# A hybrid SSD / RWKV-7 / PEER decoder step on one Trainium2 core: GpSimd's products go to VectorE

## The chip, the core and the metric

The kernel runs on one core of one Trainium2 chip. A core has TensorE (PE: matrix products into PSUM), VectorE (DVE), ScalarE (ACT), GpSimd (POOL) and SyncE (SP), which issues most transfers. The engines have queues of their own and wait for each other by semaphores. The metric is the device time of one execution in microseconds, lower is better: 3061.49 us is the median of three runs before the change (3054.85 to 3067.48).

## The reference

One layer is computed for a prompt of 512 tokens and for 8 samples of one token each, D_MODEL 1024, all in float32:

```python
h = rmsnorm(x, norm_mix)
z, xbc_raw, dt_raw, rw_proj, gate_m, gate_r = split_proj(h @ w_in)
y_m = mamba_branch(...)   # causal conv, SSD scan in chunks of 128, 32 heads, gated group norm
y_r = rwkv_branch(...)    # token shift, RWKV-7 recurrence, 16 heads of 64, group norm, bonus, gate
x = x + (sigmoid(gate_m) * y_m + sigmoid(gate_r) * y_r) @ w_out
x = x + peer(rmsnorm(x, norm_ffn))   # 8 heads, top 16 of 128 x 128 experts each, gelu
x = x + sigmoid(rmsnorm(x, norm_ple) @ w_ple_gate) * (p @ w_ple_proj)
y = rmsnorm(x, norm_final)
```

The samples start from given states (SSD, convolution, RWKV, shift); all new states are outputs too. In `peer` the top 16 of each half's scores are combined to candidates, the top 16 of those give a pair of indices (i, j) and a softmax gate, and the expert's row in `peer_u` and `peer_v` is i * 128 + j.

## The kernel before

Float32 products are made from pairs: a value is split into a part rounded for TensorE (`hi`, a copy on ACT) and the rest (`lo`, a subtraction on DVE, line 79), and `mm3` (lines 95 to 97) multiplies hi by hi, lo by hi and hi by lo. Weights arrive in tiles of 128 columns through SP's queue, are split, and meet 2 x 260 columns of tokens (512 of the prompt, 8 of the samples).

**The mixer.** A loop over eight groups g. A group is 128 RWKV channels (two of the sixteen heads) and one of the eight SSD groups (four heads, 256 channels). For each group the code projects r, k and v (`rw_tile`: raw copy on ACT, then the difference to the token before, line 418, on POOL, then the mix, line 420, on DVE); `rwkv_in` makes the decays `dr`, `di`, `dp`, `de` on ACT, normalises k to `kk` (line 545), makes `bb = kk * a` on POOL (line 547), changes `a` in place on DVE (line 548), and makes `ar`, `bk` (DVE, lines 553 to 560) and `ck` (POOL, lines 561 and 562). `rwkv_inv` multiplies `ar` by `bk` on TensorE, sends 16x16 blocks through DRAM, inverts them row by row on DVE, and reads them back into `tc16`; from it come `T16` (the buffer `di`, DVE) and `TT16` (the buffer `dp`, POOL), both on line 610. `rwkv_pre` forms the inverses of 64x64 blocks from them (its first product, line 513, reads `dp`) and the masked products `AM`; a part of `AM` is then overwritten with `ar` by copies on POOL (line 671). `rwkv_chain` is the recurrence over eight chunks of 64: each passes TensorE, DVE, TensorE, ACT, TensorE, DVE. Between these steps stand the convolution and z projections and the SSD chunks (`ssd`): its state decay (line 994) and the gating by z (line 1008) are on POOL.

**The samples** of a group are generators (`rwkv_s`, `ssd_s`) that `step()` moves on by one piece after each projection of the next group; the first group has none beside it. They load states into `sB` and `sH` and update them with products over 128x512 (lines 834 to 843) and 128x1024 (lines 916 to 921), shared between DVE and POOL. For group 7 their transfers are issued from POOL's queue (`Qu`), otherwise from SP's.

**The look-up.** `pairs` finds the pair of each of 16 candidates per head: a comparison of 128x2048 on DVE (line 1362), a product with the index table on POOL (line 1364), a sum on DVE (line 1365); twice for each of five token blocks, ten in all. The block 3 is done first; the others run as generators beside the products of the expert table `peer_u` (`u_in`, `u_out`), and `scatter` places the gates with one-hot tiles (lines 1412 and 1416, DVE). Token block 3 gathers its experts' rows by indirect transfers from POOL's queue (line 1453, five buffers), used by DVE on lines 1462 and 1468.

**Order.** A planner puts each engine's instructions in order by priorities and its own estimates. `pin` (`keep_in_program_order`) holds an instruction behind the one that was written before it for the same engine; both halves of line 610, and lines 834, 836, 916 and 917, are pinned. Each engine's queue is then fixed and runs in order.

Of the kernel before, what the change touches and what calls it, by code (L numbers as in the profile page):

```python
# [30 lines left out]
def tile_hybrid(ctx: ExitStack, tc, x_prompt, x_sample, p_prompt, p_sample, state_ssm, state_conv,  # L31
# [381 lines left out]
    def rw_tile(j):  # L413

        ps = proj(W_RW + j * P, P, hT)
        raw = raw_of(ps, rwS[:, j], rtail[:, j:j + 1], 1)
        d = l2.tile([P, 2, NH], F32, name="dtmp").rearrange("p i t -> p (i t)")[:, :512]
        G.tensor_tensor(d, raw[:, 2:514], raw[:, 3:515], op=OP.subtract)
        xs = lp.tile([P, 512], F32, name=f"xs{min(j // 8, 2)}")
        V.scalar_tensor_tensor(xs, d, rows["shift_mu"][:, j:j + 1], raw[:, 3:515], op0=OP.mult, op1=OP.add)  # L420
        return xs
# [96 lines left out]
    def rwkv_in(g, r, k, v, lw_):  # L518

        ps = pb()  # L520
        T.matmul(ps, lhsT=lw_[64:128, 1], rhs=xa[64:128], start=True, stop=True)
        a = full("a")
        S.activation(a, ps, AF.Tanh, scale=0.5, bias=rows["aaa_a0"][:, g:g + 1])
        S.activation(a, a, AF.Copy, scale=0.5, bias=0.5)
        ps = pb()
        for b in range(4):
            T.matmul(ps[:, b * P:(b + 1) * P], lhsT=xwaug[:, b * P:(b + 1) * P], rhs=lw_[0:65, 0], start=True, stop=True)
        lw = full("lw")
        S.activation(lw, ps, AF.Tanh, scale=0.5)
        S.activation(lw, lw, AF.Copy, scale=-0.5 * CDEC, bias=-0.5 * CDEC)  # L530
        dr, di, dp_, de = full("dr"), full("di"), full("dp"), full("de")
        for m, outs in ((cumI, ((dr, 1.0), (di, -1.0))), (cumS, ((dp_, 1.0),)), (cumC, ((de, 1.0),))):
            ps = pb()
            for b in range(4):
                T.matmul(ps[:, b * P:(b + 1) * P], lhsT=lw[:, b * P:(b + 1) * P], rhs=m, start=True, stop=True)
            for o, sg in outs:
                S.activation(o, ps, AF.Exp, scale=sg)
        drc = l2.tile([P, 8], F32, name="drc")
        V.tensor_copy(drc, dr[:, 63:512:64])

        sq = full("sq")
        S.activation(sq, k, AF.Square, scale=rows["k_k"][:, g:g + 1])
        ps = head_rs(sq, 1e-12, bd64, pb)
        kk = full("kk")
        V.scalar_tensor_tensor(kk, k, rows["k_k"][:, g:g + 1], ps, op0=OP.mult, op1=OP.mult)
        bb = full("bb")
        G.tensor_tensor(bb, kk, a, op=OP.mult)
        V.tensor_scalar(a, a, rows["k_a"][:, g:g + 1], omka[:, g:g + 1], op0=OP.mult, op1=OP.add)
        k2 = full("k2")
        V.tensor_tensor(k2, k, a, op=OP.mult)  # L550
        V.scalar_tensor_tensor(sq, r, rows["r_k"][:, g:g + 1], k2, op0=OP.mult, op1=OP.mult)
        ar = lp.tile([P, 8, 2, 64], F32, name="ar", bufs=2)
        V.scalar_tensor_tensor(ar[:, :, 0, :], c8(kk), -1.0, c8(dp_), op0=OP.mult, op1=OP.mult)
        V.tensor_tensor(ar[:, :, 1, :], c8(r), c8(dr), op=OP.mult)
        bk = lp.tile([P, 8, 2, 64], F32, name="bk")
        ck = lp.tile([P, 8, 2, 64], F32, name="ck")
        for e in range(2):
            sl = slice(64 * e, 64 * e + 64)
            V.tensor_tensor(bk[sl, :, e, :], c8(bb)[sl], c8(di)[sl], op=OP.mult)
            V.tensor_tensor(bk[sl, :, 1 - e, :], c8(k2)[sl], c8(di)[sl], op=OP.mult)  # L560
            G.tensor_tensor(ck[sl, :, e, :], c8(bb)[sl], c8(de)[sl], op=OP.mult)
            G.tensor_tensor(ck[sl, :, 1 - e, :], c8(k2)[sl], c8(de)[sl], op=OP.mult)
        return drc, sq, ar, bk, ck

    def bonus(sq, v):
# [8 lines left out]
    def rwkv_inv(g, ar, bk):  # L574

        L64 = c8(full("de"))
        lc16 = lp.tile([P, 8, 16], F32, name="lw")
        for hf in range(2):
            hs = slice(4 * hf, 4 * hf + 4)
            L = mm4(lambda ro, i: ar[ro, 4 * hf + i, 0, :], lambda ro, i: bk[ro, 4 * hf + i, ro.start // 64, :])  # L580
            V.tensor_tensor(L64[:, hs], L, b64(m64, 4), op=OP.mult)
            lm = c8(full("kk"))[:, 0:4]
            V.tensor_tensor(lm, L, b64(m16, 4), op=OP.mult)
            V.tensor_reduce(lc16[:, hs], lm.rearrange("p c (b k) -> p c k b", k=16), axis=AX.X, op=OP.add)
        ld, td = ld_d[g % 2], td_d[g % 2]
        nc.scalar.dma_start(ld.rearrange("c p k -> p c k"), lc16)
        yield
        lb = lp.tile([64, 16, 16], F32, name="a")
        pin(nc.sync.dma_start(lb.rearrange("q r k -> q (r k)"), ld.rearrange("c (z r) k -> (c z) (r k)", r=16)))
        yield  # L590
        tb = lp.tile([64, 16, 32], F32, name="sq")
        pin(V.memset(tb, 0.0))
        V.memset(tb.rearrange("p r k -> p (r k)")[:, 0:512:33], 1.0)
        tf = lp.tile([64, 16, 16], F32, name="k2")
        for j in range(15):
            tt = tf[:, j + 1:, 0:j + 1]
            sh = [64, 15 - j, j + 1]
            i = V.tensor_tensor(tt, lb[:, j + 1:, j:j + 1].to_broadcast(sh), tb[:, j:j + 1, 0:j + 1].to_broadcast(sh), op=OP.mult)
            if j == 0:
                pin(i)  # L600
            V.tensor_tensor(tb[:, j + 1:, 0:j + 1], tb[:, j + 1:, 0:j + 1], tt, op=OP.add)
        S.copy(tb[:, :, 16:32], tb[:, :, 0:16].rearrange("p r k -> p k r"))
        nc.scalar.dma_start(td.rearrange("c (z r) k -> (c z) (r k)", r=16), tb.rearrange("q r k -> q (r k)"))
        yield
        tc16 = lp.tile([P, 8, 32], F32, name="lw")
        pin(nc.scalar.dma_start(tc16, td.rearrange("c p k -> p c k")))
        yield
        T16, TT16 = c8(full("di")), c8(full("dp"))
        for q, (E_, t) in enumerate(((V, T16), (G, TT16))):
            pin(E_.tensor_tensor(t.rearrange("p c (b k) -> p c b k", k=16),  # L610
                                 tc16[:, :, None, 16 * q:16 * q + 16].to_broadcast([P, 8, 4, 16]),
                                 mb16[:, None].to_broadcast([P, 8, 4, 16]), op=OP.mult))
        yield L64, T16, TT16

    def rwkv_pre(g, v, ar, bk, ck, L64, T16, TT16):
# [21 lines left out]
        for hf in range(2):  # L637
# [30 lines left out]
                S.copy(uv[rv, e], pv[rv])  # L668
            for e in range(2):
                ro = slice(64 * e, 64 * e + 64)  # L670
                G.tensor_copy(AM[ro, e, :, 0:64], ar[ro, 4 * hf:4 * hf + 4, 0, :])
            out.append((AM, TT64, ctok, uv))
        return out

# [94 lines left out]
    def rwkv_s(g, lw_):  # L769
# [63 lines left out]
        yield  # L833
        pin(V.tensor_tensor(t1, sw, nkk, op=OP.mult))
        V.tensor_reduce(sa, t1, axis=AX.X, op=OP.add)
        pin(G.tensor_tensor(sw, sw, dec, op=OP.mult))
        G.tensor_tensor(t2, kS, bl(v8, 64), op=OP.mult)
        V.tensor_tensor(t1, bS, bl(sa, 64), op=OP.mult)
        V.tensor_tensor(sw, sw, t1, op=OP.add)
        V.tensor_tensor(sw, sw, t2, op=OP.add)  # L840
        Qu(g).dma_start(wkv_sample[0].rearrange("b h v k -> b (h v) k")[:, gs].rearrange("b p k -> p b k"), sw)
        G.tensor_tensor(t2, sw, rS, op=OP.mult)
        V.tensor_reduce(yrS[:, g], t2, axis=AX.X, op=OP.add)

    def samples_out(l2):
# [31 lines left out]
    def ssd_s(g):  # L877
# [33 lines left out]
        for i in range(2):  # L911
# [1 line left out]
            hs_, t1 = (lp.tile([P, 8, P], F32, name="sH", bufs=2) for _ in range(2))  # L913
            pin(Qu(g).dma_start(hs_, sst[:, rs_].rearrange("b p n -> p b n")))
            yield
            pin(G.tensor_tensor(t1, Bb, bl(dx[:, i, 0:8], P), op=OP.mult))
            pin(V.tensor_tensor(hs_, hs_, bl(dx[:, i, 8:16], P), op=OP.mult))
            V.tensor_tensor(hs_, hs_, t1, op=OP.add)
            Qu(g).dma_start(sso[:, rs_].rearrange("b p n -> p b n"), hs_)
            G.tensor_tensor(t1, hs_, Cb, op=OP.mult)  # L920
            V.tensor_reduce(y2[:, i], t1, axis=AX.X, op=OP.add)
            if i == 0:
                yield
# [18 lines left out]
    def ssd(g, xt, bm, cm, sz):  # L942
# [9 lines left out]
        for c in range(4):  # L952
# [38 lines left out]
            T.matmul(ps[:, 0:256], lhsT=bt, rhs=xde, start=True, stop=True)  # L991
            st2 = l2.tile([P, 256], F32, name="sst")
            if c:
                G.tensor_tensor(v4(st2), v4(st), hb(elast, c), op=OP.mult)
                V.tensor_tensor(st2, st2, ps[:, 0:256], op=OP.add)
            else:
                S.copy(st2, ps[:, 0:256])
# [7 lines left out]
        nc.scalar.dma_start(ssm_prompt[0, 0].rearrange("h q n -> (h q) n")[g * 256:(g + 1) * 256].rearrange("(j p) n -> p j n", p=P), so)  # L1005

        for j in range(2):
            G.tensor_tensor(yf[j], yf[j], sz[j], op=OP.mult)
            S.activation(sz[j], yf[j], AF.Square)
        V.tensor_tensor(sz[0], sz[0], sz[1], op=OP.add)  # L1010
        yield
# [309 lines left out]
    def pairs(pool, c, gate):  # L1321
# [38 lines left out]
        for s_ in range(2):  # L1360
            eq = pool.tile([P, 8, 16, 16], F32, name="eq")[:n]
            V.tensor_tensor(eq, iota[:n, None, None, 0:16].to_broadcast([n, 8, 16, 16]),
                            ab[:, s_].unsqueeze(3).to_broadcast([n, 8, 16, 16]), op=OP.is_equal)
            G.tensor_tensor(eq, eq, fi[:, :, s_].unsqueeze(2).to_broadcast([n, 8, 16, 16]), op=OP.mult)
            V.tensor_reduce(ij[:, s_].rearrange("p (h k) -> p h k", h=8), eq, axis=AX.X, op=OP.add)
            yield
        V.tensor_tensor(gate, top, top[:, :, 0:1].to_broadcast([n, 8, 16]), op=OP.subtract)
# [349 lines left out]
```

## Time and profile before

| what | value |
|---|---|
| median of three runs | 3061.49 us |
| the profiled execution | 3051.57 us |
| its span, first to last instruction | 3049.9 us |
| TensorE busy, mean granted clock | 2821.5 us (93%), 0.954 |
| DVE busy | 2249.9 us (74%) |
| ACT busy | 988.6 us (32%) |
| POOL busy | 685.8 us (22%), 309.6 of it indirect transfers |

The granted clock is the share of TensorE's full clock that the chip allowed in a stretch. The mixer runs from the start to about 1200 us, the branch and output projections to about 1430, scores and look-up keys to 1560, the products with `peer_u` to about 2400, those with `peer_v` to 2954, and the last block to the end. Busy shares are means over stages with different limits.

### The profile page before, as it was taken

The page shows a single profiled execution, that of the slowest core. Times are in us where ns is not written, and L with a number is a line of the kernel's source. Part 1 is how long each engine was busy: PE and PEld are TensorE (multiplying, and loading weights), DVE is VectorE, ACT ScalarE, POOL GpSimd, SP SyncE. Part 2 cuts the span into 40 slices and gives each one's busy share as a digit, 9 for nine tenths or more (in the row PEclk, how much of TensorE's full clock was granted, in tenths as well). Part 3 has the DMA queues.
Part 4 walks back from the last instruction along what each step waited for, and adds up shares of the span by engine and source line. Part 5 has one row for each costly group of instructions (what it writes and reads, how often), then busy time and mean ns, then how long its engine had stood idle before and what let it go on. Part 6 is the DMA issues. An engine that isn't in the chain of part 4 may idle for free. (4 is left out here: it accounts for less than half of the span.)

```text
span 3049.9 us, 52517 instructions
## 1 busy us (share of the span) xinstructions
PE 2821.5 (93%) x20188; PEld 2617.4 (86%) x20192; DVE 2249.9 (74%) x5375; ACT 988.6 (32%) x1995; POOL 685.8 (22%) x522
## 2 busy tenths in 40 slices
PE   5999999898897999998968989899999999999998
PEld 4878888777777888987968989898999999999986
DVE  5867767787777775334999999695677778878846
ACT  2333323333242322332223333232323343333332
POOL 0222231322314132210013121121222333432100
PEclk9999979998988999999989999999999999999999
DMA  3314242424334265632326768677998989988830
GB/s 87 78 41 105 76 103 60 113 60 104 73 87 113 68 153 158 198 112 93 90 61 198 245 203 245 211 241 230 315 334 303 328 302 327 337 326 313 287 119 29
DMA packets 446995, 528.15 MB, mean 173 GB/s; under 512 B 95464, under 2 KB 357243, under 8 KB 446705
## 3 DMA queue, kind: packets, MB, share of 16 engines
q1 hardware_dynamic: 386153, 377.42, 40.1%
q0 software_dynamic: 38304, 139.22, 13.5%
q10 hardware_dynamic: 22288, 8.16, 1.1%
q8 instruction: 159, 2.61, 0.4%
q14 instruction: 91, 0.75, 0.1%
HBM read 447.83 MB, written 77.14 MB: 172 GB/s over the span
## 5 line engine op out<-in xcount | busy, mean ns | idle before, releaser
L97 PE MATMUL ps<-hhi,wlo 128*128 128x260 f32 (+1 forms) x1456 | 444.6, 305 | 1.7 <-DVE wlo L79 1.7
L96 PE MATMUL ps<-hlo,whi 128*128 128x260 f32 (+1 forms) x1456 | 444.4, 305 | 0.0
L95 PE MATMUL ps<-hhi,whi 128*128 128x260 f32 (+1 forms) x1456 | 443.8, 305 | 0.6 <-DVE rsa L122 0.3
L97 PE MATMUL psA<-h2h,ul 128*128 128x392 f32 x1024 | 354.1, 346 | 24.8 <-DVE ul L1500 24.4
L95 PE MATMUL psA<-h2h,uh 128*128 128x392 f32 x1024 | 365.7, 357 | 0.2 <-ACT uh L1499 0.2
L96 PE MATMUL psA<-h2l,uh 128*128 128x392 f32 x1024 | 354.6, 346 | 0.0
L97 PE MATMUL av<-ah,vl 128*128 128x392 f32 x1024 | 351.5, 344 | 1.9 <-DVE vl L79 1.9
L95 PE MATMUL av<-ah,vh 128*128 128x392 f32 x1024 | 348.9, 341 | 3.3 <-ACT vh L78 3.2
L96 PE MATMUL av<-al,vh 128*128 128x392 f32 x1024 | 349.6, 341 | 0.9 <-DVE al L79 0.9
L95 PEld LDWEIGHTS ps<-hhi,whi 128*128 128x128 f32 (+1 forms) x1456 | 286.6, 197 | 13.9 <-issue 6.8
L96 PEld LDWEIGHTS ps<-hlo,whi 128*128 128x128 f32 (+1 forms) x1456 | 286.6, 197 | 12.7 <-issue 6.0
L97 PEld LDWEIGHTS ps<-hhi,wlo 128*128 128x128 f32 (+1 forms) x1456 | 286.3, 197 | 12.6 <-issue 4.0
L1453 POOL DMA_INDIRECT gr<-in_peer_v_dram,e x128 | 184.3, 1440 | 367.9 <-DVE o L1468 349.7
L1453 POOL DMA_INDIRECT gr<-in_peer_u_dram,e x128 | 125.3, 979 | 499.8 <-DVE junk L1462 448.2
L78 ACT CAST vh<-vr 128x1024 fp32r<-128x1024 f32 x128 | 134.3, 1051 | 315.8 <-PE av L96 121.3
L97 PEld LDWEIGHTS psA<-h2h,ul 128*128 128x128 f32 x1024 | 196.7, 192 | 27.4 <-DVE ul L1500 26.3
L78 ACT CAST whi<-wraw 128x1024 fp32r<-128x1024 f32 (+1 forms) x115 | 119.9, 1043 | 292.9 <-PE ps L96 250.5
L95 PEld LDWEIGHTS psA<-h2h,uh 128*128 128x128 f32 x1024 | 196.7, 192 | 0.9 <-ACT uh L1499 0.9
L96 PEld LDWEIGHTS psA<-h2l,uh 128*128 128x128 f32 x1024 | 197.3, 193 | 0.0
L79 DVE TENSOR_TENSOR vl<-vr,vh 128x1024 fp32r<-128x1024 f32 x128 | 156.2, 1222 | 55.4 <-ACT vh L78 52.2
L95 PEld LDWEIGHTS av<-ah,vh 128*128 128x128 f32 x1024 | 192.9, 188 | 3.9 <-ACT vh L78 3.5
L97 PEld LDWEIGHTS av<-ah,vl 128*128 128x128 f32 x1024 | 192.9, 189 | 2.5 <-DVE vl L79 2.5
(635 smaller groups left out, 6498.9 us busy)
## 6 DMA issues: line engine op xcount, KB each, us to landing
ur<-in_peer_u_dram SPq DMA_DIRECT2D x128, 512.0 KB
vr<-in_peer_v_dram SPq DMA_DIRECT2D x128, 512.0 KB
wraw<-in_w_in_dram SPq DMA_DIRECT2D x90, 512.0 KB
Gt<-G_d SPq DMA_DIRECT2D x32, 784.0 KB
G_d<-stg SPq DMA_DIRECT2D x12, 2048.0 KB
ge_d<-ge SPq DMA_DIRECT2D x112, 196.0 KB
gl<-ge_d SPq DMA_DIRECT2D x112, 196.0 KB
wraw<-in_w_out_ssm_dram SPq DMA_DIRECT2D x16, 512.0 KB
```

The source lines that it names most:

```text
L78: S.copy(hi, raw)
L79: eng.tensor_tensor(lo, raw, f(hi), op=OP.subtract)
L95: T.matmul(out, lhsT=a[0], rhs=b[0], start=start, stop=False)
L96: T.matmul(out, lhsT=a[0], rhs=b[1], start=False, stop=False)
L97: T.matmul(out, lhsT=a[1], rhs=b[0], start=False, stop=stop)
L1453: pin(G.indirect_dma_start(out=t, out_offset=None, in_=(peer_u, peer_v)[s_ // P][0], in_offset=bass.IndirectOffsetOnAxis(ap=e3[:, s_ % P:s ...
```

## The change

Products and differences that were issued to POOL (`G`) are issued to DVE (`V`) with the same operands, in the same places of the program; the copies of `ar` into `AM` go to ACT (`S`). What was pinned stays pinned, now behind DVE's instruction before it. POOL keeps the indirect transfers, the transfers of group 7's samples, the masks of the set-up, the subtraction of line 1143 for every second tile and the split of the mixed output (`split(..., G)`).

```diff
@@ rw_tile
-        G.tensor_tensor(d, raw[:, 2:514], raw[:, 3:515], op=OP.subtract)
+        V.tensor_tensor(d, raw[:, 2:514], raw[:, 3:515], op=OP.subtract)
@@ rwkv_in
-        G.tensor_tensor(bb, kk, a, op=OP.mult)
+        V.tensor_tensor(bb, kk, a, op=OP.mult)
...
-            G.tensor_tensor(ck[sl, :, e, :], c8(bb)[sl], c8(de)[sl], op=OP.mult)
-            G.tensor_tensor(ck[sl, :, 1 - e, :], c8(k2)[sl], c8(de)[sl], op=OP.mult)
+            V.tensor_tensor(ck[sl, :, e, :], c8(bb)[sl], c8(de)[sl], op=OP.mult)
+            V.tensor_tensor(ck[sl, :, 1 - e, :], c8(k2)[sl], c8(de)[sl], op=OP.mult)
@@ rwkv_inv
-        for q, (E_, t) in enumerate(((V, T16), (G, TT16))):
+        for q, (E_, t) in enumerate(((V, T16), (V, TT16))):
@@ rwkv_pre
-                G.tensor_copy(AM[ro, e, :, 0:64], ar[ro, 4 * hf:4 * hf + 4, 0, :])
+                S.copy(AM[ro, e, :, 0:64], ar[ro, 4 * hf:4 * hf + 4, 0, :])
@@ rwkv_s
-        pin(G.tensor_tensor(sw, sw, dec, op=OP.mult))
-        G.tensor_tensor(t2, kS, bl(v8, 64), op=OP.mult)
+        pin(V.tensor_tensor(sw, sw, dec, op=OP.mult))
+        V.tensor_tensor(t2, kS, bl(v8, 64), op=OP.mult)
...
-        G.tensor_tensor(t2, sw, rS, op=OP.mult)
+        V.tensor_tensor(t2, sw, rS, op=OP.mult)
@@ ssd_s
-            pin(G.tensor_tensor(t1, Bb, bl(dx[:, i, 0:8], P), op=OP.mult))
+            pin(V.tensor_tensor(t1, Bb, bl(dx[:, i, 0:8], P), op=OP.mult))
...
-            G.tensor_tensor(t1, hs_, Cb, op=OP.mult)
+            V.tensor_tensor(t1, hs_, Cb, op=OP.mult)
@@ ssd
-                G.tensor_tensor(v4(st2), v4(st), hb(elast, c), op=OP.mult)
+                V.tensor_tensor(v4(st2), v4(st), hb(elast, c), op=OP.mult)
...
-            G.tensor_tensor(yf[j], yf[j], sz[j], op=OP.mult)
+            V.tensor_tensor(yf[j], yf[j], sz[j], op=OP.mult)
@@ pairs
-            G.tensor_tensor(eq, eq, fi[:, :, s_].unsqueeze(2).to_broadcast([n, 8, 16, 16]), op=OP.mult)
+            V.tensor_tensor(eq, eq, fi[:, :, s_].unsqueeze(2).to_broadcast([n, 8, 16, 16]), op=OP.mult)
```

## Rows read from the trace of the kernel before

**Rows 1.** The page: busy us, share of the span and instructions of each engine.
```profile
PE 2821.5 (93%) x20188; PEld 2617.4 (86%) x20192; DVE 2249.9 (74%) x5375; ACT 988.6 (32%) x1995; POOL 685.8 (22%) x522
```
**Rows 2.** Stages: length, PE, PEld, DVE, ACT, POOL busy (count), clock, DMA share, GB/s.
```profile
105.00:1200.00 1095.00, 1004.04 (x8871) 872.74 (x8873) 811.40 (x2022) 363.24 (x929) 285.82 (x211) 0.92 0.37 92
105.00:219.00 114.00, 108.82 (x1038) 94.09 (x1039) 81.05 (x212) 44.74 (x114) 20.27 (x18) 0.99 0.20 55
357.00:505.00 148.00, 139.27 (x1156) 120.43 (x1156) 108.83 (x266) 49.25 (x131) 35.07 (x25) 0.88 0.34 84
850.00:863.00 13.00, 10.19 (x73) 8.84 (x72) 11.46 (x17) 4.78 (x13) 7.72 (x5) 0.50 0.44 121
1200.00:1375.00 175.00, 166.83 (x1289) 152.84 (x1289) 71.94 (x139) 60.52 (x96) 31.87 (x29) 0.97 0.51 156
1660.00:1900.00 240.00, 226.94 (x1484) 224.41 (x1483) 230.92 (x672) 85.62 (x158) 52.41 (x38) 0.97 0.73 230
```
**Rows 3.** TensorE's waits, 105 to 1200 us: total us, times, longest.
```profile
PE psB L513 <- POOL dp L610: 23.2, 6, 6.7
PE psB L513 <- DVE bk L559: 22.8, 13, 3.2
```
**Rows 4.** Timeline around `bk` of one group: start, us, engine, line, idle before.
```profile
358.30 2.14 POOL L547 TENSOR_TENSOR bb<-kk,a 128x512 f32<-128x512 f32 x1 [25.57 <-DVE kk L545]
360.48 1.62 DVE L548 TENSOR_SCALAR a<-a,VB,omka 128x512 f32<-128x512 f32 x1 [1.18 <-POOL bb L547]
364.29 0.67 DVE L559 TENSOR_TENSOR bk<-bb,di 64x512 f32<-64x512 f32 x1
365.02 0.64 PE L513 MATMUL psB<-bk,ar 64*64 64x64 f32 x4 [2.89 <-DVE bk L559]
```
**Rows 5.** Timeline around `dp` of a later group.
```profile
829.68 0.69 DVE L610 TENSOR_TENSOR di<-lw,mb 128x512 f32<-128x512 f32 x1
836.66 1.26 POOL L610 TENSOR_TENSOR dp<-lw,mb 128x512 f32<-128x512 f32 x1
837.97 1.97 PE L513 MATMUL psB<-dp,de 64*64 64x64 f32 x32 [6.69 <-POOL dp L610]
```
**Rows 6.** POOL by line: busy us, mean ns, idle before and its releasers.
```profile
L418 POOL TENSOR_TENSOR dtmp<-raw 128x512 f32<-128x512 f32 x26 | 41.6, 1600 | 149.0 <-ACT raw L408 77.0 <-ACT rwS L409 35.7 <-ACT rtail L410 25.3
L920 POOL TENSOR_TENSOR sH<-sH,sB 128x1024 f32<-128x1024 f32 x16 | 40.0, 2498 | 94.2 <-DVE sH L918 86.5 <-DVE bonA L813 7.7
L1364 POOL TENSOR_TENSOR eq<-eq,fi 128x2048 f32<-128x2048 f32 x8 | 37.1, 4635 | 263.2 <-DVE eq L1362 263.2
L916 POOL TENSOR_TENSOR sH<-sB,s_dx 128x1024 f32<-128x1024 f32 x16 | 31.3, 1956 | 6.0 <-DMA out_dram<-sH 2.9 <-DMA sB<-bc_d 2.7
```
**Rows 7.** DVE and ACT by line, shapes apart, the prices.
```profile
L1010 DVE TENSOR_TENSOR sz<-sz,sz 128x512 f32<-128x512 f32 x8 | 5.5, 687 | 3.3 <-ACT sz L1009 3.3
L918 DVE TENSOR_TENSOR sH<-sH 128x1024 f32<-128x1024 f32 x16 | 19.5, 1218 | 0.0
L995 DVE TENSOR_TENSOR sst<-sst,psA 128x256 f32<-128x256 f32 x24 | 9.9, 414 | 1.4 <-PE psA L991 1.2
L1362 DVE TENSOR_TENSOR eq<-iota,ab 128x2048 f32<-128x2048 f32 x8 | 18.2, 2281 | 0.0
L559 DVE TENSOR_TENSOR bk<-bb,di 64x512 f32<-64x512 f32 x16 | 19.1, 1196 | 0.2
L668 ACT COPY uv<-psB 64x256 f32<-64x256 f32 x32 | 11.7, 366 | 10.5 <-PE psB L665 10.2
L602 ACT COPY sq<-sq 64x256 f32<-64x256 f32 x8 | 5.3, 661 | 6.8 <-DVE sq L601 6.8
```
**Rows 8.** Timeline of the look-up: POOL's product, DVE beside it and after.
```profile
1739.65 4.90 POOL L1364 TENSOR_TENSOR eq<-eq,fi 128x2048 f32<-128x2048 f32 x1 [6.55 <-DVE eq L1362]
1740.03 5.38 DVE L1416 TENSOR_SCALAR o<-iota,tT 128x128 f32<-128x128 f32 x4
1748.28 1.10 DVE L1416 TENSOR_SCALAR o<-iota,tT 128x128 f32<-128x128 f32 x4
```

## The prediction

> **What bounds the kernel now.** I read the page's busy line first, then stages, then waits, then the instructions at the waits. The page gives TensorE 93% of the span, DVE 74%, POOL 22% [rows 1]: TensorE bounds the kernel, and a change to DVE and POOL counts only where TensorE waits for them or where its clock falls. The chain of waits reaches back only into the last 52 us, after everything the change touches, so it can't tell the price and the stages must.
>
> The stage with nearly all the moved work is the eight-group mixer, 105 to 1200 us. There TensorE is busy 1004.0 of 1095 us and its mean granted clock is 0.92 [rows 2]. So 91 us are idle, and the lower level (1.2 of 2.4 GHz) costs up to 1095 x (1 - 0.92) = 88 us more. The first group, which carries no samples yet, took 114 us at clock 0.99; a later one, with a sample group beside it, took 148 us at 0.88 [rows 2]. TensorE's waits in this stage have two large entries: 23.2 us for POOL's `dp` (line 610) and 22.8 us for DVE's `bk` (line 559), half of the idle time [rows 3].
>
> Both come from POOL. At `bk`: after `kk`, POOL's `bb` took 2.14 us; DVE's in-place step on `a` (line 548) had to wait for it, then took 1.62 us; the first `bk` came at 364.29, and TensorE had stood 2.89 us [rows 4]. At `dp`: DVE made `di` at 829.68, but `dp`, made from the same loaded tile, stood in POOL's queue behind the samples' products and began at 836.66; TensorE stood 6.69 us [rows 5]. Behind that wait the clock was 0.50 between 850 and 863 us, in the recurrence [rows 2].
>
> The other stage is the expert look-up, where DVE is the crowded engine: 230.9 of 240 us between 1660 and 1900, beside TensorE's 226.9 [rows 2].
>
> **The change part by part.** All against the profiled run's 3051.57 us (span 3049.9).
>
> DVE's new work in the mixer, by counts in the code: 82 products of 128x512 (26 of line 418, 8 of 547, 8 of 610, 24 of 836, 837 and 842, 16 of 1008) at 0.687 us are 56.3; 32 of `ck`, 64x512, at 0.67 are 21.4; 32 of the state, 128x1024, at 1.218 are 39.0; 24 of 128x256 at 0.414 are 9.9 [rows 4, 7]. Sum 127 us. POOL pays about twice that: 1.60 and 2.50 us for the first and the third of these [rows 6].
>
> What DVE gets back: its instructions are held while POOL computes. The `bk` of line 559 takes 1.196 us in the mean, where one alone takes 0.67: 16 of them lost 19.1 - 10.7 = 8.4 us [rows 4, 7]. That one line is the lower bound of the relief; the upper one is all of POOL's 285.8 us [rows 2]. The same reading (mean less shortest of a form) over all DVE lines of the stage, of which this is among the largest, comes to about 80 us, and I take that. DVE so grows by 47, from 811 to 858 us [rows 2].
>
> The Trainium skill, page "SBUF — State Buffer", section "SBUF: two separate sides", calls this an exclusive lock: a DVE instruction with two SBUF inputs and a GpSimd one that reads SBUF shut each other out for the whole instruction. By that rule the relief could come near all of POOL's arithmetic and DVE would even end up less busy; the four 5.38 us of [rows 8] agree with the mechanism, but most DVE instructions of the mixer here met no POOL one, so I stay with the measured sum.
>
> (a) `dp` moves directly behind `di` on DVE, held there in program order, and ends some 0.7 us after it: about 831.0; TensorE ran dry at 837.97 - 6.69 = 831.3 [rows 5]. All 23 us go. If the planner lets the samples' products between, nothing goes: 0 to 23, I take 23. Late next is the recurrence itself.
>
> (b) `bb` on DVE costs 0.69 instead of 2.14 us, and the steps behind it are no longer held; the first `bk` of [rows 4] then comes about 3 us earlier, as much as TensorE waited. If the four `ck` go ahead of it (4 x 0.62 = 2.5 us), nearly nothing is won: 3 to 23, I take 19.
>
> (c) The clock. Part of the 88 us comes back if the waits that precede the low stretches go; part belongs to the recurrence's small matmuls. 0 to 88; the nearest row is the first group, without such waits on POOL and at 0.99 [rows 2], but it has no samples beside it, so I take a third, 29.
>
> (d) DVE's 47 us of net growth. DVE is idle 1095 - 811 = 284 us there, which hides most. Without that cover all 47 are on the path, as the recurrence's three DVE steps per chunk queue behind products of up to 1.2 us. 0 to 47, I take a third: -16. The subtraction of line 418, the state's decay (994) and the gating (1008) get quicker one by one; they have no large wait of TensorE behind them, so I count nothing. The pinned product 916 now waits on DVE for its loads and for a store that frees its buffer; in POOL's queue the sixteen of them waited 6.0 us [rows 6], which bounds this cost at 6 us, and it is inside (d).
>
> (e) The 32 copies into `AM` go to ACT, not to DVE. The nearest rows are 0.366 us (64x256 from PSUM) and 0.661 us (64x256 in SBUF) [rows 7]: 12 to 21 us on an engine busy 363 of 1095 us [rows 2]. The cover is gone only where the recurrence's first matmul waits for them, say 0.6 us a group; 0 to 21, I take -5.
>
> Mixer: 23 + 19 + 29 - 16 - 5 = 50 us won.
>
> (f) The look-up's ten products: POOL 4.64 us each; on DVE as much as the comparison of the same shape, 2.281 us, ten of them 22.8 us [rows 6, 7]. While one ran, four DVE instructions took 5.38 us together that otherwise take 1.10: 4.28 us lost against 2.28 added, 2.0 won each [rows 8]. Ten give 20 us of DVE. Where the planner had other work for DVE that POOL didn't hold, nothing is won and 22.8 is lost: -23 to +20; TensorE feels about half, I take 10.
>
> The gathers in POOL's queue lose the products between them; they have five buffers and wait mostly for DVE's use of the rows, so nothing is counted. The stage from 1200 to 1375 keeps POOL's 31.9 us [rows 2]: line 1143 and the split of the mixed output are not touched, so the change's words say a little more than it does.
>
> Sum: 60 us, 3051.57 - 60 = 2991.6. The profiled run lies 9.9 us under the median of the three shown (3061.49); with half of that, **2997 us**, on its own 2960 to 3035.
>
> **The rivals.**
>
> R1: the waits go, the clock doesn't come back. For it: the low stretch at 850 lies in the recurrence, whose small matmuls stay; against it: the first group has the same recurrence at 0.99 [rows 2]. 60 - 29 = 31 won: 3026.
>
> R2: nearly all the clock's loss comes back, as in the first group: 59 us more: 2937. Against it: the samples' steps stay between.
>
> R3, slower: DVE becomes what the mixer waits for. Moved `ck`, `dp` and sample products stand ahead of `bk`, of the weight splits and of the chunk steps; (a), (b) and (c) bring nothing, and the 47 + 5 us are all on the path, less 10 of the look-up: +42, with the same 5 us 3098. It decides once DVE is over some 90% busy in a group, as between 1660 and 1900, where 96% went with 13 us of idle TensorE [rows 2]. Against it: 858 us in a stage of 1045 is 82%.
>
> R4: the look-up pays in full. DVE has 9 us left between 1660 and 1900 [rows 2], so 22.8 us are added there and none given back, while the mixer wins its 50: 3051.57 - 27 + 5 = 3029. Against it: [rows 8]. The Trainium skill, page "Perfetto Trace Analysis", section "Optimizing Scalar/DVE Operations", speaks for R4: it would move work off a saturated DVE, even to GpSimd, though it adds that the shared port may spoil that.
>
> R5: the change doesn't do what it says where it counts: the planner puts `dp` and the first `bk` behind other DVE work, late as before, and relief and new work cancel: about 3051.
>
> **How the numbers follow.** Forecast 0.47, R1 0.15, R2 0.11, R3 0.14, R4 0.06, R5 0.07. The range 2935 to 3070 leaves out R3 and the far end of R2. About 0.5% (15 us) is what a measurement of this kernel tells from no change; slower is R3, 0.14; no change is R5 with the upper edges of R1 and R4, 0.12; faster is the rest, 0.74.
>
> **What would show it.** (a) TensorE's wait for line 610 gone, and DVE's `dp` within a microsecond of `di`. (b) its wait for line 559 under 5 us. (c) the mixer's granted clock at 0.94 or more. (d) DVE near 858 us in the mixer with `bk` at 0.67; `bk` still at 1.2 would refute the relief. (f) line 1416 without any 5 us stretch, and 1660 to 1900 shorter. The forecast is wrong if the mixer takes 1095 us or more, or if new TensorE waits for DVE of over 30 us stand in the place of the two.

## The result: 2.4% faster, two thirds of it in the mixer, one third in the look-up

The changed kernel took 2985.28 us in the median of four runs (2977.0 to 2992.63), the kernel before 3058.17 beside it: ratio 0.9763 [0.9727, 0.98]. The forecast was 2997 us, on its own 2960 to 3035. The profiled execution took 2980.14 us with a span of 2978.4, against 3051.57 and 3049.9.

**Where the time went.** First the page's busy line of the kernel after, which answers to [rows 1].

```profile
PE 2785.6 (94%) x20189; PEld 2594.3 (87%) x20192; DVE 2243.9 (75%) x5555; ACT 1001.0 (34%) x2027; POOL 350.2 (12%) x310
```

POOL lost 335.6 us. DVE got 180 instructions more and is 6 us *less* busy.

Then the stages, cut at the same instructions in both kernels: the mixer from the first group's `kk` to the first output projection, and the stretch of the look-up from the first tile of `peer_u` to the 80th. The columns are those of [rows 2]. Before:

```profile
104.60:1211.60 1107.00, 1013.07 (x8931) 879.38 (x8935) 820.67 (x2076) 367.75 (x938) 285.82 (x211) 0.92 0.37 93
1568.30:2153.10 584.80, 524.87 (x3358) 517.30 (x3356) 492.25 (x1350) 193.51 (x359) 128.36 (x92) 0.95 0.68 217
```

After, with the stage between them that keeps POOL's 31.9 us:

```profile
101.50:1161.80 1060.30, 990.29 (x8929) 864.81 (x8932) 821.47 (x2241) 380.78 (x970) 11.98 (x14) 0.92 0.39 97
1161.80:1340.00 178.20, 171.02 (x1291) 156.94 (x1291) 71.39 (x106) 60.38 (x94) 31.68 (x29) 0.98 0.53 158
1518.80:2080.80 562.00, 513.35 (x3357) 507.96 (x3356) 484.56 (x1360) 193.13 (x359) 82.43 (x82) 0.96 0.71 225
```

The mixer's end came 1211.6 - 1161.8 = 49.8 us earlier, the look-up took 22.8 less; together 72.6 of the span's 71.5. The other stages stayed within 1 us. In the mixer of these two executions the granted clock is 0.92 both times, and DVE, with 165 instructions more, is as busy as before.

**The two waits.** TensorE's waits in the mixer after, columns as in [rows 3]:

```profile
PE psB L513 <- DVE dp L610: 15.4, 4, 6.7
PE psB L655 <- DVE AM L647: 7.5, 8, 2.3
PE psB L717 <- ACT uv L713: 7.4, 14, 0.5
```

The wait for `bk` has gone altogether, the one for `dp` only by a third. From the timeline at `bk` of the group of [rows 4] (rows in between left out):

```profile
358.29 0.75 DVE L545 SCALAR_TENSOR_TENSOR kk<-xs,VB,psB 128x512 f32<-128x512 f32 x1 [0.84 <-PE psB L493]
359.21 0.68 DVE L547 TENSOR_TENSOR bb<-kk,a 128x512 f32<-128x512 f32 x1
360.41 0.54 DVE L548 TENSOR_SCALAR a<-a,VB,omka 128x512 f32<-128x512 f32 x1
360.87 0.68 DVE L559 TENSOR_TENSOR bk<-bb,di 64x512 f32<-64x512 f32 x1
362.50 0.44 PE L513 MATMUL psB<-bk,ar 64*64 64x64 f32 x4
```

`bb` takes 0.68 us, the step on `a` 0.54 where it took 1.62, and from the start of `bb` to that of `bk` it takes 1.66 us instead of the 5.99 of [rows 4]. At `dp` (answers to [rows 5], another group; lines 836 and 837 left out):

```profile
663.06 0.69 DVE L610 TENSOR_TENSOR di<-lw,mb 128x512 f32<-128x512 f32 x1 [5.03 <-DMA lw<-td_d]
663.67 0.68 DVE L835 TENSOR_REDUCE s_sa<-sH 128x8 f32<-128x512 f32 x1
665.47 0.68 DVE L838 TENSOR_TENSOR sH<-sB,s_sa 128x512 f32<-128x512 f32 x1
666.07 0.68 DVE L610 TENSOR_TENSOR dp<-lw,mb 128x512 f32<-128x512 f32 x1
666.81 1.44 PE L513 MATMUL psB<-dp,de 64*64 64x64 f32 x22 [6.35 <-DVE dp L610]
```

Here `dp` starts 3.0 us after `di`, with the samples' steps between, instead of 7.0 in [rows 5]. Directly behind `di` it would have started 2.4 us earlier, so 2.4 of TensorE's 6.35 us are the samples' steps. DVE itself stood idle 5.03 us before `di`, for the transfer that brings the inverted blocks back (`lw<-td_d`), and the other 3.95 us hang on that. Over the four waits left, some 5 of 15.4 us are the steps' by the same reckoning and some 10 the transfer's.

**What came back as other waits.** The recurrence's own steps (line 655 feeds them), TensorE's lines by what ended the idle time before them (last column), before:

```profile
L717 PE MATMUL psB<-uv,ctok 128*64 128x64 f32 x256 | 22.2, 251 | 1.5 <-ACT uv L713 1.5
L711 PE MATMUL psB<-X,TT 64*64 64x64 f32 x256 | 22.0, 250 | 2.6 <-DVE X L707 2.6
L703 PE MATMUL psB<-uv,AM 128*64 128x64 f32 x224 | 19.2, 251 | 1.7 <-DVE uv L723 0.9 <-DVE uv L692 0.8
L655 PE MATMUL psB<-identf,ck 64*128 64x64 f32 x128 | 17.4, 272 | 3.7 <-DVE AM L647 1.9 <-ACT ctok L657 1.6
```

and after:

```profile
L717 PE MATMUL psB<-uv,ctok 128*64 128x64 f32 x256 | 23.5, 267 | 7.4 <-ACT uv L713 7.4
L711 PE MATMUL psB<-X,TT 64*64 64x64 f32 x256 | 23.5, 265 | 7.7 <-DVE X L707 5.8 <-ACT uv L668 1.9
L703 PE MATMUL psB<-uv,AM 128*64 128x64 f32 x224 | 21.0, 271 | 5.2 <-DVE uv L723 4.0 <-DVE uv L692 1.2
L655 PE MATMUL psB<-identf,ck 64*128 64x64 f32 x128 | 18.3, 280 | 12.3 <-DVE AM L647 7.5 <-ACT ctok L657 4.6
```

These four waited 9.5 us before and 32.6 after. So beside the 30.6 us that the two waits of [rows 3] lost (46.0 - 15.4), the recurrence's own waits grew by 23.1 (a new order alone made them 16.5, see the controls below); other, smaller waits went, and TensorE's idle time in the mixer fell by 1107.0 - 1013.1 = 93.9 to 70.0, that is 24 us. The other 23 of the mixer's 47 us are TensorE's busy time (1013.1 to 990.3): the trace's clock records put 174 us before and 164 after at the lower level (1.2 of 2.4 GHz; "half clock" below), worth about 5 by their length, or 12 by TensorE's busy time inside them (158 and 134 us). The rest stays open.

**DVE's prices** after, columns as in [rows 7], with the line of the look-up:

```profile
L559 DVE TENSOR_TENSOR bk<-bb,di 64x512 f32<-64x512 f32 x16 | 10.9, 682 | 0.1
L916 DVE TENSOR_TENSOR sH<-sB,s_dx 128x1024 f32<-128x1024 f32 x16 | 19.5, 1220 | 2.1 <-DMA sB<-bc_d 1.1 <-DMA out_dram<-sH 0.9
L1364 DVE TENSOR_TENSOR eq<-eq,fi 128x2048 f32<-128x2048 f32 x8 | 18.3, 2284 | 0.0
L1416 DVE TENSOR_SCALAR o<-iota,tT 128x128 f32<-128x128 f32 x392 | 111.5, 340 | 14.3 <-PE gs L1395 14.0
```

`bk` costs 0.682 us instead of 1.196 [rows 7], and line 1416 has a mean of 340 ns where before it had 381:

```profile
L1416 DVE TENSOR_SCALAR o<-iota,tT 128x128 f32<-128x128 f32 x392 | 128.1, 381 | 13.7 <-PE gs L1395 13.5
```

TensorE's waits in the look-up's stretch, before:

```profile
PE psA L97 <- DVE ul L1500: 24.4, 4, 18.7
PE tr L1498 <- DMA ur<-in_peer_u_dram: 18.2, 6, 6.0
PE gs L1395 <- DVE o L1416: 9.6, 5, 4.4
PE gs L1384 <- DVE ij L1365: 6.1, 1, 6.1
PE gs L1385 <- DVE ij L1365: 1.2, 1, 1.2
```

and after:

```profile
PE tr L1498 <- DMA ur<-in_peer_u_dram: 25.2, 9, 6.4
PE psA L97 <- DVE ul L1500: 21.6, 2, 21.2
PE gs L1384 <- DVE ij L1365: 1.7, 1, 1.7
```

The waits for one-hot tiles and indices have gone from 16.9 to 1.7 us; the table's own transfers and the long wait at its first tiles stay. Half of the stretch's 22.8 us is TensorE's idle time (59.9 to 48.6 us), half its busy time, and of that half most can be the clock: half clock took 61 us before and 44 after, worth about 9.

### The profile page after: what moved, and what is told of

Its sections match the earlier page's. It is cut to its first block, busy times and chain, and to the rows that moved or that the text cites. A ratio compares the mean times of both kernels' runs of the same rounds, so it can differ in the third digit from the quotient of the medians.

```text
span 2978.4 us, 52286 instructions
## 1 busy us (share of the span) xinstructions
PE 2785.6 (94%) x20189; PEld 2594.3 (87%) x20192; DVE 2243.9 (75%) x5555; ACT 1001.0 (34%) x2027; POOL 350.2 (12%) x310
## 5 line engine op out<-in xcount | busy, mean ns | idle before, releaser
L1453 POOL DMA_INDIRECT gr<-in_peer_v_dram,e x128 | 177.5, 1387 | 375.3 <-DVE o L1468 357.7
```

Source lines behind the costliest of these rows:

```text
L1453: pin(G.indirect_dma_start(out=t, out_offset=None, in_=(peer_u, peer_v)[s_ // P][0], in_offset=bass.IndirectOffsetOnAxis(ap=e3[:, s_ % P:s ...
```

## Experiments

Three theories of the mixer's gain stood against each other. **Q**: a result that TensorE needs comes late because it stands in POOL's queue or takes POOL's long time; DVE's queue is the shorter way. **H**: POOL's arithmetic holds DVE, and every us of it that goes is worth something. **P**: the planner, given other costs, puts everything in another order, and the gain is that order's. The look-up has its own pair: DVE held (gain), or DVE loaded (R4, loss).

Ratios are to the kernel before on the same chip with 95% intervals. Of each trace two things come back below: the mixer's length, cut as above (1107.0 before), and its two waits (23.2 and 22.8). The length is of one execution: against the ratio's time it is off by up to 11 us (the second control below), so the ratio decides.

**One part alone.** `dp` only:

```diff
-        for q, (E_, t) in enumerate(((V, T16), (G, TT16))):
+        for q, (E_, t) in enumerate(((V, T16), (V, TT16))):
```

> The kernel before with one product moved: dp (line 610) on DVE behind di. Theory Q (TensorE waited for POOL's queue): dp comes 7 to 9 us earlier in groups 1 to 6, TensorE's wait for line 610 falls from 23.2 us to about 12 (what is left hangs on the read-back), mixer 12 to 25 us shorter, ratio 0.992 to 0.996; DVE's busy time in the mixer hardly changes (+0 to +4 us). Theory H (the gain is DVE no longer held by POOL's arithmetic): all of POOL's other work stays, so the mixer gains under 5 us, ratio 0.998 to 1.002. Theory P (a planner's reordering, no single cause): any sign, up to 15 us.

0.9933 [0.991, 0.9956]: 20 us. Its waits:

```profile
PE psB L513 <- DVE bk L559: 23.6, 10, 3.2
```

That for `dp` is down to 1.5 us, that for `bk` stays, and the mixer took 1093.3 us. From `kk` to the first product with `dp`, the groups 1 to 6 together took 297 us instead of 341 (292 in the full change, 330 and 331 in the two controls below). TensorE's idle time in the mixer fell by 9.8 us only (93.9 to 84.1), and the four lines of the recurrence waited 23.2 us instead of 9.5.

`bb` and `ck`, together and each alone:

```diff
-        G.tensor_tensor(bb, kk, a, op=OP.mult)
+        V.tensor_tensor(bb, kk, a, op=OP.mult)
...
-            G.tensor_tensor(ck[sl, :, e, :], c8(bb)[sl], c8(de)[sl], op=OP.mult)
-            G.tensor_tensor(ck[sl, :, 1 - e, :], c8(k2)[sl], c8(de)[sl], op=OP.mult)
+            V.tensor_tensor(ck[sl, :, e, :], c8(bb)[sl], c8(de)[sl], op=OP.mult)
+            V.tensor_tensor(ck[sl, :, 1 - e, :], c8(k2)[sl], c8(de)[sl], op=OP.mult)
```

> The kernel before with bb and the four ck products (lines 547, 561, 562) on DVE. Theory Q: TensorE's wait for bk (22.8 us) falls under 6 us, bk comes 2 to 3 us earlier after kk in each of eight groups, mixer 15 to 22 us shorter, ratio 0.992 to 0.996. Theory H: bk's mean falls from 1.2 to 0.67 us; POOL loses 64 of its 274 us of the mixer, so a quarter of the 50 us: 12 us. They differ in DVE's busy time: under H the 27 us of new work are paid back in full (+0), under a relief by half +13.

0.9887 [0.9863, 0.9911]: 35 us. The wait for `bk` is gone, that for `dp` grew:

```profile
PE psB L513 <- POOL dp L610: 35.5, 6, 8.2
```

DVE was busy 811.2 us in the mixer, 9.5 *less* than before with 27 us of products more, so that some 35 us of holding went.

> The kernel before with bb alone (line 547) on DVE; ck stays on POOL, where it now starts as early and still holds DVE's steps before bk. Theory Q (latency of POOL's results): bk comes 2 us earlier, the wait for bk falls from 22.8 to about 8 us, mixer 12 to 18 us shorter, ratio 0.994 to 0.996. Theory H (DVE held by POOL): only 13 of POOL's 274 us go; bk's mean stays at 1.2 us; under 4 us, ratio 0.9985 to 1.

> The kernel before with the 32 ck products alone (lines 561, 562) on DVE; bb stays on POOL. Theory H: bk's mean falls to about 0.7 us, DVE's 22 us of new work are paid back, the first bk is no longer held and the mixer is 15 to 25 us shorter, ratio 0.992 to 0.995. Theory Q: bb still takes its 1.3 to 2.1 us on POOL and TensorE waits for bk as before (18 to 23 us); the mixer gains under 5 us, ratio 0.998 to 1.

Only `bb`: 0.9922 [0.9897, 0.9947]; `bk` waits 12.8 us. Only `ck`, of which `bk` uses nothing: 0.9918 [0.9893, 0.9944], and yet

```profile
PE psB L513 <- DVE bk L559: 5.6, 8, 1.1
```

The price of `bk` on DVE tells the two apart; with only `bb` moved, and with only `ck` moved:

```profile
L559 DVE TENSOR_TENSOR bk<-bb,di 64x512 f32<-64x512 f32 x16 | 18.4, 1151 | 0.2
```

```profile
L559 DVE TENSOR_TENSOR bk<-bb,di 64x512 f32<-64x512 f32 x16 | 10.9, 683 | 0.1
```

In the group of [rows 4] it was not `bk` but the steps ahead of it that `ck` held before (in the kernel after, line 548 takes 0.54 us and line 553 0.69):

```profile
360.52 2.69 POOL L561 TENSOR_TENSOR ck<-bb,de 64x512 f32<-64x512 f32 x2
362.02 1.75 DVE L553 SCALAR_TENSOR_TENSOR ar<-kk,dp 128x512 f32<-128x512 f32 x1
```

So the `bk` wait had two causes: `bb`'s latency and, the larger one, the holding of `bk` and of the steps up to it by `ck`, which ran beside them on POOL. In this place H holds. Either part alone wins some 70% of what both win. With only `bb` moved, though, TensorE's idle time in the mixer did not fall (98.4 us): what that part won in its trace lies in TensorE's busy time, with 130 us at half clock instead of 174.

The samples' five products:

```diff
-        pin(G.tensor_tensor(sw, sw, dec, op=OP.mult))
-        G.tensor_tensor(t2, kS, bl(v8, 64), op=OP.mult)
+        pin(V.tensor_tensor(sw, sw, dec, op=OP.mult))
+        V.tensor_tensor(t2, kS, bl(v8, 64), op=OP.mult)
...   (and the same on lines 842, 916 and 920)
```

> The kernel before with the samples' five products on DVE (lines 836, 837, 842, 916, 920). It takes 104 us of POOL's 274 in the mixer and clears the queue in front of dp, but leaves bb. Theory Q: the wait for line 610 falls under 14 us, that for bk stays at 20 or more; mixer 12 to 25 us shorter, as e1_dp. Theory H: 104 of 274 us of holding go, 20 us; DVE's busy time in the mixer stays within 8 us though 55 us of products are added. Both near 0.993; DVE's busy time and the two waits tell them apart.

0.9927 [0.9906, 0.9948]: 22 us, and `dp`'s wait fell though `dp` stayed on POOL, since the samples' products no longer stood ahead of it there:

```profile
PE psB L513 <- DVE bk L559: 25.4, 11, 3.2
PE psB L513 <- POOL dp L610: 5.0, 3, 3.8
```

DVE was 17 us busier (838.1), where H expected at most 8.

What prediction and theory had counted at nothing, lines 418, 994, 1008 to DVE and 671 to ACT:

```diff
-        G.tensor_tensor(d, raw[:, 2:514], raw[:, 3:515], op=OP.subtract)
+        V.tensor_tensor(d, raw[:, 2:514], raw[:, 3:515], op=OP.subtract)
...
-                G.tensor_copy(AM[ro, e, :, 0:64], ar[ro, 4 * hf:4 * hf + 4, 0, :])
+                S.copy(AM[ro, e, :, 0:64], ar[ro, 4 * hf:4 * hf + 4, 0, :])
...   (and G to V on lines 994 and 1008)
```

> The kernel before with what the prediction counted at nothing: lines 418, 994 and 1008 on DVE, and the AM copies of line 671 on ACT. Theory Q: no large wait of TensorE hangs on them: -5 to +5 us, ratio 0.998 to 1.0015. Theory H: 105 of POOL's 274 us in the mixer go, so 10 to 19 us shorter, ratio 0.994 to 0.997.

0.9884 [0.9858, 0.9909]: 35 us, as much as `bb` and `ck` together and more than Q or H allows. Both waits are still there:

```profile
PE psB L513 <- POOL dp L610: 30.1, 7, 10.0
PE psB L513 <- DVE bk L559: 22.0, 9, 3.1
```

The mixer took 1075.6 us, 31.4 less, of which TensorE's idle time makes 4.0 (93.9 to 89.9) and its busy time the rest. Half clock took 130 us instead of 174, worth 22 by its length and up to 28 by TensorE's busy time inside it. So most of this gain can be the clock's; what raised the clock isn't shown, and P isn't excluded here. The experiment missed its expectation, and its cause stays open. TensorE's waits for ACT were 10.1 us in this mixer (9.3 before), so that the copies on ACT cost nothing that can be seen.

The look-up's product:

```diff
-            G.tensor_tensor(eq, eq, fi[:, :, s_].unsqueeze(2).to_broadcast([n, 8, 16, 16]), op=OP.mult)
+            V.tensor_tensor(eq, eq, fi[:, :, s_].unsqueeze(2).to_broadcast([n, 8, 16, 16]), op=OP.mult)
```

> The kernel before with the look-up's ten products (line 1364) on DVE. Theory H: each product held DVE for most of 4.6 us and costs 2.28 there, so products with peer_u shorten by 20 to 25 us, as in the full change (585 to 562 us); mixer unchanged; ratio 0.992 to 0.994. The prediction's term (f), half of 20 felt: 10 us, 0.997. The rival R4 (DVE saturated, no relief): 15 to 23 us longer, 1.005 to 1.0075.

0.9939 [0.9921, 0.9956]: 18.7 us, with the mixer unchanged. Its stretch from the first to the 80th tile:

```profile
1568.60:2130.00 561.40, 511.88 (x3356) 506.68 (x3355) 483.91 (x1356) 192.95 (x358) 82.73 (x82) 0.97 0.70 226
```

561.4 us, as in the full change (562.0; before 584.8): this part is independent of the rest. R4 is refuted, on an engine that is busy 86% of the stretch.

**Place without work.** The test that parts Q from H and P: nothing changes its engine; `dp`, still on POOL, is only no longer pinned behind the samples' products written before it.

```diff
-            pin(E_.tensor_tensor(t.rearrange("p c (b k) -> p c b k", k=16),
+            (pin if q == 0 else lambda i: i)(E_.tensor_tensor(t.rearrange("p c (b k) -> p c b k", k=16),
```

> The kernel before, nothing moved to another engine; only dp is no longer held in program order on POOL, so that it stands ahead of the samples' products in POOL's queue. Theory Q (a place in a queue): dp follows di within 2 us, the mixer is 10 to 20 us shorter as with dp on DVE, ratio 0.992 to 0.996. Theory H (POOL's arithmetic holds DVE): POOL does the same work, 274 us: no gain, 0.998 to 1.002. Theory P (any other order of the planner helps, since the one before was a poor one): a gain of 0.5 to 1% too; the two control kernels of this call tell P from Q.

0.9942 [0.9924, 0.9961]: 18 us, beside 20 for moving it. The timeline of one group, and the waits:

```profile
802.83 1.44 POOL L610 TENSOR_TENSOR dp<-lw,mb 128x512 f32<-128x512 f32 x1 [15.70 <-DMA lw<-td_d]
803.07 1.75 DVE L610 TENSOR_TENSOR di<-lw,mb 128x512 f32<-128x512 f32 x1
```

```profile
PE psB L513 <- DVE bk L559: 21.9, 9, 3.2
PE psB L513 <- POOL dp L610: 5.0, 5, 2.2
```

POOL's `dp` now starts with `di` (each holds the other a little: 1.44 and 1.75 us) and the wait is down to 5 us, with POOL busy 278 us in the mixer (286 before). From `kk` to the first product with `dp` the groups 1 to 6 took 292 us, as in the full change. So `dp` was late by its place in POOL's queue, not by its engine. How the 18 us follow from that is not shown: TensorE's idle time fell by 6.7 us only, and half clock took 119 us instead of 174.

**Order without the change.** Two controls change only the planner's priority of the weights' splits:

```diff
-        with tc.high_priority(300):
+        with tc.high_priority(1000):
```

and, in the second, 100.

> Control: the kernel before, no instruction on another engine, only the priority of the weight splits raised from 300 to 1000, which changes the planner's order on TensorE in thousands of places. Theories Q and H: POOL's queue and its holding stay, -6 to +10 us, ratio 0.998 to 1.003. Theory P: 15 to 25 us shorter, 0.992 to 0.995, as every single part of the change was.

> Control: as the one before with the priority lowered to 100. Theories Q and H: 0.998 to 1.003. Theory P: 0.992 to 0.995.

1.0016 [1.0006, 1.0026] and 0.9971 [0.9956, 0.9985], although a line-by-line comparison of TensorE's order in the traces finds 1967 and 1588 lines changed (2391 with the unpinned `dp`, 3107 in the full change). These two new orders moved the time by 0.2 and 0.3%, the second a little more than Q and H allow; the smallest part above is 0.58%. Two draws don't bound what an order can do, and the interval of the second touches that of the unpinned `dp`. P so is no likely cause of any part as a whole, but may be in each with some 9 us (half of what the unpinned `dp` won), so differences of that size between parts mean nothing. In the first control the four lines of the recurrence waited 16.5 us and in the second 14.0, so that only values well above these tell of more than order.

**On top of the full change.** What POOL still does in the next stage (line 1143 and the split of the mixed output) goes to DVE too:

```diff
-            (G if k % 2 else V).tensor_tensor(lo[:, k, :, 0:256], t, f(hi[:, k, :, 0:256]), op=OP.subtract)
+            V.tensor_tensor(lo[:, k, :, 0:256], t, f(hi[:, k, :, 0:256]), op=OP.subtract)
...
-                split(gt[:, :, w_], v2(mhi), v2(mlo), G)
+                split(gt[:, :, w_], v2(mhi), v2(mlo), V)
```

> The changed kernel with the last arithmetic of POOL (line 1143 and the split of the mixed output) on DVE too. DVE's instructions between the mixer and the keys then lose their 35 us of holding and gain 15 us of work. Both theories say that this stage doesn't hang on DVE (72 of 175 us busy, TensorE 167): same time as the changed kernel, 2975 to 2995 us, ratio to the kernel before 0.973 to 0.979. If holding by itself were the price, it would win 20 us more: 0.970.

0.9754 [0.9729, 0.9779], not to be told from the full change. The stage:

```profile
1166.00:1345.00 179.00, 173.86 (x1307) 159.44 (x1305) 83.55 (x142) 62.19 (x97) 0.24 (x1) 0.98 0.53 161
```

179.0 us against 178.2, with DVE 12 us busier: where TensorE waits for DVE only 2.7 us in all, the work may lie on either.

And the full change with the samples' five products back on POOL (the diff of the third experiment, reversed, on the kernel after):

> The changed kernel with the samples' five products back on POOL (104 us of it); dp, bb and ck stay on DVE, so nothing that TensorE waited for stands in POOL's queue. Theory H: DVE is held again for most of 104 us, its busy time in the mixer stays near 820 us though 55 us of products left it, and the mixer loses 10 to 25 us against the changed kernel: ratio to the kernel before 0.980 to 0.985. Theory Q: as the changed kernel or a little better, as DVE has less to do: 0.973 to 0.978.

0.974 [0.9723, 0.9756], 2977.65 us, the best measured, though not to be told from the full change. In the mixer

```profile
102.70:1150.50 1047.80, 981.09 (x8927) 854.85 (x8931) 802.08 (x2185) 379.08 (x969) 113.47 (x70) 0.95 0.40 98
```

POOL computes 101 us again (the row counts 12 us of issued transfers too), and DVE, freed of 55 us of products, is only 19 us less busy: it is held for some 36 us. That costs no time, and TensorE is idle no longer than in the full change (66.7 and 70.0 us). The clock was higher here, though (next table), so a small price of the holding could hide behind it. The 10 to 25 us that H expected did not come: POOL's arithmetic harms where it stands ahead of, or beside, what TensorE waits for.

**The clock over all executions.** The stages above are of one execution each, but every execution has its mean granted clock over the whole kernel. The last column takes the time that the lower level can have cost, time x (1 - clock), from that of the kernel before on the same chips; it is an upper bound, as TensorE is idle in part of that time.

| kernel | won by ratio, us | TensorE idle in the mixer, us | mean clock | clock gave back at most, us |
|---|---|---|---|---|
| before (50 executions) | | 93.9 | 0.953 (0.948 to 0.957) | |
| `dp` on DVE | 20 | 84.1 | 0.960 | 24 |
| `bb` and `ck` | 35 | 83.3 | 0.957 | 15 |
| `bb` | 24 | 98.4 | 0.959 | 16 |
| `ck` | 25 | 86.7 | 0.954 | 4 |
| samples' products | 22 | 89.5 | 0.962 | 28 |
| the rest (418, 994, 1008, 671) | 35 | 89.9 | 0.961 | 24 |
| `dp` unpinned | 18 | 87.2 | 0.964 | 37 |
| control 1000 | -5 | 100.1 | 0.955 | 8 |
| control 100 | 9 | 96.4 | 0.955 | 10 |
| full change (4) | 72 | 70.0 | 0.957 | 17 |
| samples back on POOL | 80 | 66.7 | 0.962 | 35 |

So the waits are only part of what the parts won. Where `dp` no longer came late, by whichever of three ways, the mean clock rose to 0.960 to 0.964; but it rose as much with "the rest", where both waits stood, so that what raises it stays open.

**The parts don't add up.** In the mixer they win 20 + 35 + 22 + 35 = 112 us alone and 47 to 50 together. By pairs this is seen too: `bb` and `ck` alone 0.78% and 0.82%, both 1.13%. One reason is that `dp` alone, the samples and the unpinned `dp` remove the same wait by three ways. The traces put the larger part elsewhere: TensorE's idle time fell by 9.8 + 10.6 + 4.4 + 4.0 = 28.8 us alone and by 23.9 together, which nearly adds up, while its busy time fell by 63.2 us alone and by 22.8 together, and the clock gave back more with three of the four parts alone than with all of them. The recurrence's own waits (9.5 us before, 23.2 with `dp` alone, 23.8 with the samples, 32.6 in the full change) are why its idle time falls by less than the two waits do.

## Why the prediction was right

The time came 12 us under the forecast, well inside its range, and the split into mixer (50 forecast, 50 by its end) and look-up (10, 23) was nearly right. But the mixer's 50 came out by luck: the terms that make it up were wrong in both directions.

(a) `dp` behind `di`: 23 forecast; alone it won 20, and 18 by its place alone, of which TensorE's idle time makes 9.8 and 6.7. The sign "`dp` within a microsecond of `di`" did not appear: in the full change only 8 us of the wait went. In three of the groups 1 to 6 the planner put four of the samples' steps between (`dp` starts 3.0 us after `di`), the case priced at nothing, in the others one (1.2 us); the read-back holds the rest.

(b) `bk`: 19 forecast, the wait's 22.8 gone in full, 35 won alone, up to 15 of it the clock's. `ck` did not queue ahead of `bk`; on POOL it had been holding `bk` and the steps up to it, which the term left out.

(c) The clock: 29 forecast, 5 to 12 found in the mixer's trace, where the granted clock stayed 0.92 and not 0.94; over all executions of the whole kernel at most 17. This is the step that failed in size. The low stretches lie in the recurrence with or without the wait ahead of it: with `dp` moved alone, TensorE did not wait for the products with `dp` at 684, 817 and 950 us, and 9 us behind each the clock fell for 17 to 20 us. The first of them:

```profile
693.00:710.00 17.00, 12.26 (x92) 10.62 (x93) 13.51 (x18) 6.46 (x16) 7.06 (x6) 0.50 0.73 207
```

R1's "for" (the recurrence's small matmuls stay) was the better reading of that trace. That the mean clock did rise over all executions with the `dp` wait gone (table above) speaks for a part of the forecast's step; the share isn't shown.

(d) DVE's net growth: 47 forecast, 0.8 measured. Without the moved instructions DVE is busy 719.0 us in the mixer after, 820.7 before: a relief of 101.7 where the sum has 80. "Mean less shortest", taken over every line and shape of the stage, gives 128 and not about 80. The moved ones, 127 us in the sum and 123 by their own rows, add only 102.5, as neighbouring rows of DVE overlap (0.68 us long, they start 0.60 us apart in the timeline at `di` above). The rule of the Trainium skill, page "SBUF — State Buffer", section "SBUF: two separate sides" (a DVE instruction with two SBUF inputs and a GpSimd one that reads SBUF, or a DVE one in a 2-port mode and any GpSimd one, exclude each other for the whole instruction), was nearer: DVE ended no busier, though the relief is 102 of POOL's 274 us of arithmetic and not nearly all of it. Rows with one tensor input (lines 548 and 1416) were held too, which only the 2-port half of that rule could cover; the prediction left it out, and no view shows an instruction's mode. Part by part the relief runs from nothing (`dp` alone: DVE 7.4 us busier for 5.5 of products) through a third (some 36 of 101 us with the samples back) to half (some 35 of 66 for `bb` and `ck`). Of the -16 nothing is seen in DVE's sum, but TensorE's waits for DVE in the recurrence's four lines grew by 12 us. All its waits for DVE and POOL in the mixer fell, from 82.9 to 42.3 us, so that the sign of a wrong forecast (over 30 us of new waits for DVE) stayed away, if not by much: 15.4 for `dp` and these 12.

(e) ACT's copies: ACT is 13 us busier, as forecast (12 to 21). TensorE's waits for ACT in the same four lines grew by 11 us; that is not the copies' doing, for with the copies on ACT and the samples on POOL ("the rest") its waits for ACT in the mixer were 10.1 us, and with the samples on DVE and the copies on POOL 21.3. The -5 was not seen.

(f) The look-up: 10 forecast, 23 in the stretch and 18.7 by ratio. The size was off: DVE's busy time fell by 7.7 us only (30.5 of holding gone, 22.8 added), less than the 20 forecast, and the stage paid three times that. TensorE felt not half of DVE's sum but the places: its waits for line 1416's tiles and for `ij`, 16.9 us before, are 1.7 after, and the granted clock rose from 0.95 to 0.96 (0.97 with this part alone). The page "Perfetto Trace Analysis" of the Trainium skill, section "Optimizing Scalar/DVE Operations", spoke for R4 where it would move work off a saturated engine, even to GpSimd; here the engine at 96% between 1660 and 1900 [rows 2] gained by taking work back. Its reservation, that the shared port may spoil such a move, is what the row of line 1416 shows (381 ns before, 340 after).

What I counted at nothing: line 1143's stage, rightly; lines 418, 994 and 1008, wrongly when alone (35 us with the copies, most of it possibly the clock's), and in the full change not separable.

## What to carry over

Before moving work off an engine because it is slow, look at what stands ahead of the needed result in that engine's queue: letting `dp` go first on POOL won as much as giving it to DVE. Holding of DVE by POOL is real, but here it was paid where TensorE waited behind it, so it is read at the waits and not from busy sums. And a part's gain is split into TensorE's idle and busy time before it is put down to a wait: here the idle time of the parts nearly added up, and what the clock gave back did not.

## What the runs showed of the hardware

- DVE's busy time can fall when work is added to it: 811.2 us against 820.7 in the mixer with 32 products of 64x512 and 8 of 128x512 more that POOL no longer did.
- In the kernel after, a product costs DVE half of what it cost POOL before: 1.220 us for 128x1024 (POOL 2.498) and 2.284 us for 128x2048 (POOL 4.635) [rows 6].
- TensorE's time at half clock in the mixer ran from 106 us (samples back on POOL) to 174 (before) between kernels with nearly the same matmuls, and also between the two controls that moved no work (160 and 133). One trace says little of a kernel here: the mean clock of the kernel before ran from 0.948 to 0.957 over 50 executions, that is 55 us at half clock. The means over executions (table above) differ by more than that between some kernels, and neither of the two waits alone predicts them; what does stays open.
